# First-layer rows loaded one group ahead on another queue, one normalisation moved, one warm-up product added

## The chip, the cores and the metric

One core of a Trainium2 chip runs the whole program. The metric is device microseconds of one execution; the median of the runs counts. Engines and queues are named as in the profile: PE is TensorE, PEld its weight loads, DVE is VectorE, ACT is ScalarE, POOL is GpSimd, SP is SyncE, which here only starts transfers. A transfer is started from SP's queue or from ACT's queue.

## The reference

A two-layer encoder on 256 tokens of width 2048, all in float32:

```
for l in range(DEPTH):                                   # DEPTH = 2
    h = rms_norm(x, norm1_g[l])
    q, k, v, gu, gv = jnp.split(h @ w_in[l], splits, axis=-1)
    q = apply_rope(rms_norm(q, q_norm_g[l]), cos, sin)   # 8 query heads of 128
    k = apply_rope(rms_norm(k, k_norm_g[l]), cos, sin)   # 2 key/value heads
    attn = banded_window_attention(q, k, v, sink[l])
    sgu = chunked_spatial_gating(gelu(gu), gelu(gv), sgu_ln_g[l], sgu_ln_b[l], w_s[l], b_s[l])
    mixed = concatenate([rms_norm(attn, attn_out_g[l]), rms_norm(sgu, sgu_out_g[l])], axis=-1)
    x = x + mixed @ w_o[l]
    x = x + conv_gated_ffn(rms_norm(x, norm2_g[l]), w_up[l], conv_w[l], conv_b[l], w_down[l])
```

The RMS norms divide each row by the root of its mean square. Since that factor is one number per row, the kernel multiplies the unscaled rows by the weights and applies the factor to the product.

## The kernel before

Each product is made from three: an operand is split into a high part, rounded to a shorter float32 format, and a low part, the rest; high times high, low times high and high times low are added up in PSUM. Weights arrive by SP's queue in blocks of 1 MB (`raw`, three buffers), ACT makes the high part (`hi`, L128) and DVE the low part (`lo`, L110), each in two halves of 128x1024, with four half buffers each. PE needs one block for 24 products of 512 columns.

The work around the change has three places.

**The start.** `first_rows(b)` (L510) makes the operands of one of four groups of rows of the transposed input `xT`: for group 0 from the two tiles `xs` loaded at the very start, for groups 1 to 3 from two tiles of 256 KB that it loads itself on SP's queue (L515). ACT makes the high part of each 128-row piece (L246) and DVE its low part (L247). The first layer's loop at L548 calls it for group b and then multiplies that group with two weight blocks, one of the keys and values (`psk`) and one of the first four query heads (`psq`). I number the weight blocks 0, 1, 2 and so on; group b meets blocks 2b and 2b+1. Before the first weights land, PE multiplies a constant tile with itself nine times (L97, `WARM`). In group 1 ACT's queue loads the rotary tables `ropes` (L555), the norm gains `qk` (L334) and the column parameters `pc` (L335), in group 2 the residual `xr` in two halves of 1 MB (L559). In the last group DVE makes the rotary tables times gains (L343, L345) and the negated sinks (L353), and ACT sums the squares of the residual (L306).

**The attention half's norm.** `inv_rms_cols(acca, ...)` (L287) adds the sums of squares of the attention output on DVE (L288), and puts a piece of work called `turned` on a list. `let_in` takes such a piece off the list at a fixed point of the next block of products: it turns the sums with two PE transposes (L294), reduces them on DVE (L296), and POOL takes the power. It is called at L681, between the first and second unit of the gating half (`gated(0)` and `gated(1)`), so `let_in` of `gated(1)` takes it in. Its result `ra` is used by the first residual of the output projection (L530).

**The spatial products.** `spatial(u)` (L653) uses a PSUM buffer of the same two-buffer pool (`tp`) as the attention's transposes and L294.

What sets the order: the program is written out once, a scheduler orders each engine's instructions by readiness and priority (`urgent` raises it, `issue_after` binds a piece behind a named instruction), and on the chip each engine runs its own list in that order. Transfers use eight completion semaphores in turn, so a transfer may wait for the landing of the one that last used its semaphore.

## Time and profile before

| | |
|---|---|
| Median of 3 runs | 2008.98 us (2008.42 to 2009.18) |
| Profiled execution: its time, its span | 2008.75 us, 2007.0 us |
| PE busy | 2000.7 us (100%) |
| DVE busy | 1367.1 us (68%) |
| ACT busy | 1068.1 us (53%) |
| Transfers | 382.22 MB, mean 190 GB/s |
| First 10 us, 10 to 20 us, 20 to 30 us | 239, 413, 411 GB/s |

The span runs from the first instruction of the program to the last; the profiled execution took 1.75 us more than its span. A row of the timeline gives start and duration in us, engine, line, operation, tiles, count, and in brackets the idle time of the engine before it and what ended that. Blocks of rows that follow one another on an engine are merged.

### The profile page before, as it was taken

How to read it: one execution, taken by the hardware profiler on the slowest of the kernel's cores; microseconds unless marked ns; L12 is line 12 of the kernel's file. 1: busy time of each engine (PE TensorE's matmuls, PEld its weight loads, DVE VectorE, ACT ScalarE, POOL GpSimd, SP SyncE). 2: the span in 40 equal slices, each digit the busy share in tenths (PEclk: the TensorE clock that was granted, in tenths of full speed). 3: DMA queues.
4: the chain of work that ended last, by engine and by line, in shares of the span. 5: the costliest groups of instructions: out<-in, count | busy, mean ns of one | idle time of the engine just before them, and what ended most of it. 6: DMA issues, size and time to landing. Idle time of an engine off the chain costs nothing.

```text
span 2007.0 us, 26356 instructions
## 1 busy us (share of the span) xinstructions
PE 2000.7 (100%) x10426; PEld 1718.6 (86%) x10426; DVE 1367.1 (68%) x1866; ACT 1068.1 (53%) x1460; POOL 20.4 (1%) x25
## 2 busy tenths in 40 slices
PE   9999999999999999999999999999999999999999
PEld 7888888888888888888888888888888888888887
DVE  6878666777755577775567786667777444777753
ACT  6576465555543455555455764655555334555532
POOL 0100000000000000000000000000000000000000
PEclk9999999999999999999999999999999999999999
DMA  8644645455555544555556355544555554455563
GB/s 336 228 147 147 209 157 200 168 181 214 205 198 189 186 171 171 211 209 189 189 186 231 127 173 187 182 173 169 210 208 192 194 199 172 168 194 208 207 210 126
DMA packets 58011, 382.22 MB, mean 190 GB/s; under 512 B 6688, under 2 KB 7968, under 8 KB 12832
## 3 DMA queue, kind: packets, MB, share of 16 engines
q1 hardware_dynamic: 56880, 377.72, 53.2%
q10 hardware_dynamic: 1008, 2.83, 0.4%
q8 instruction: 81, 1.33, 0.3%
q14 instruction: 42, 0.34, 0.0%
HBM read 378.43 MB, written 2.10 MB: 190 GB/s over the span
## 4 chain that ended last, share of the span: by engine, by line
PE 97%; DMA 2%; DVE 1%; issue 0%; ACT 0%; SPq 0%; POOL 0%; DVEq 0%; ACTq 0%
PE mm L166 40%; PE mm L225 30%; PE mm L231 16%; PE mm L202 4%; PE mm L207 2%; PE tp L166 1%; DMA raw<-in_w_in 1%; PE tp L501 1%; DMA sl<-in_xT 1%; PE tp L463 0%; PE tp L266 0%; PE tp L653 0%; DVE lo L110 0%; PE tp L268 0%; PE tp L267 0%
## 5 line engine op out<-in xcount | busy, mean ns | idle before, releaser
L110 DVE TENSOR_TENSOR lo<-raw,hi 128x1024 fp32r<-128x1024 f32 (+1 forms) x708 | 840.5, 1215 | 445.1 <-ACT hi L128 287.6
L128 ACT ACTIVATE hi<-raw 128x1024 fp32r<-128x1024 f32 (+1 forms) x708 | 732.6, 1051 | 673.0 <-PE mm L166 374.3
L166 PE MATMUL mm<-hi,sl 128*128 128x512 f32 x2480 | 668.0, 391 | 0.7 <-ACT sl L246 0.7
L225 PE MATMUL mm<-sl,hi 128*128 128x512 f32 x2688 | 617.8, 389 | 0.0
L225 PEld LDWEIGHTS mm<-sl,hi 128*128 128x128 f32 x2688 | 501.8, 188 | 103.4 <-ACT hi L128 1.0
L166 PEld LDWEIGHTS mm<-hi,sl 128*128 128x128 f32 x2480 | 463.9, 188 | 96.4 <-ACT sl L246 1.1
L166 PE MATMUL mm<-lo,sl 128*128 128x512 f32 x1240 | 382.9, 390 | 0.0
L231 PEld LDWEIGHTS mm<-sl,lo 128*128 128x128 f32 x2688 | 328.1, 192 | 3.3
L231 PE MATMUL mm<-sl,lo 128*128 128x256 f32 x2688 | 329.1, 283 | 0.0
L166 PEld LDWEIGHTS mm<-lo,sl 128*128 128x128 f32 x1240 | 232.5, 188 | 48.1
L731 DVE SCALAR_TENSOR_TENSOR sc<-ev,pc,sc 128x255 f32<-128x255 f32 x176 | 80.9, 481 | 87.4 <-ACT sc L730 87.4
L239 ACT COPY ev<-mm 128x512 f32<-128x512 f32 x96 | 55.4, 577 | 130.6 <-PE mm L231 114.8
L730 ACT ACTIVATE sc<-ev,pc 128x256 f32<-128x256 f32 x176 | 98.9, 589 | 0.0
L202 PE MATMUL mm<-sl,hi 128*128 128x512 f32 x384 | 92.8, 392 | 0.0
L734 DVE SCALAR_TENSOR_TENSOR sc<-ev,pc,sc 128x255 f32<-128x255 f32 x176 | 80.9, 481 | 3.0
L202 PEld LDWEIGHTS mm<-sl,hi 128*128 128x128 f32 x384 | 70.8, 188 | 13.8
L254 ACT ACTIVATE sl<-sl 128x256 fp32r<-128x256 f32 x88 | 31.8, 409 | 68.3 <-DVE sl L751 68.3
L241 DVE TENSOR_TENSOR ev<-mm,ev 128x512 f32<-128x512 f32 x96 | 65.7, 684 | 0.0
L726 DVE TENSOR_TENSOR ev<-ev,rb 128x512 f32<-128x512 f32 x88 | 60.1, 683 | 0.2
L207 PE MATMUL mm<-sl,lo 128*128 128x256 f32 x384 | 50.4, 284 | 0.0
L207 PEld LDWEIGHTS mm<-sl,lo 128*128 128x128 f32 x384 | 48.3, 191 | 0.9
L255 DVE TENSOR_TENSOR sl<-sl 128x256 fp32r<-128x256 f32 x88 | 33.5, 421 | 20.1 <-ACT sl L254 20.1
(122 smaller groups left out, 692.3 us busy)
## 6 DMA issues: line engine op xcount, KB each, us to landing
raw<-in_w_up SPq DMA_DIRECT2D x176, 1024.0 KB, 5.1
raw<-in_w_down SPq DMA_DIRECT2D x88, 1024.0 KB, 4.8
raw<-in_w_in SPq DMA_DIRECT2D x38, 1024.0 KB, 5.0
raw<-in_w_o SPq DMA_DIRECT2D x32, 1024.0 KB, 4.9
raw<-in_w_gu SPq DMA_DIRECT2D x16, 1024.0 KB, 4.8
sl<-in_prow SPq DMA_DIRECT2D x12, 256.0 KB, 6.2
raw<-in_w_in SPq DMA_DIRECT2D x8, 256.0 KB, 5.2
xr<-in_x ACTq DMA_DIRECT2D x2, 1024.0 KB, 8.8
```

Source lines behind the costliest of these rows:

```text
L110: nc.vector.tensor_tensor(out=lo, in0=part, in1=hi.bitcast(F32), op=ALU.subtract)
L128: nc.scalar.activation(hi[:, cs], part, AF.Copy)
L166: nc.tensor.matmul(ps[m], acts[kk][:, part % 2, m * P : (m + 1) * P], w, start=first and kk == 0 and part == 0, stop=last and kk == KB - 1 ...
L202: nc.tensor.matmul(ps[:, i, :], tile_of(his, k, i), x1, start=k == 0, stop=False)
L207: nc.tensor.matmul(ps[:, i, :SEQ], tile_of(los, k, i), acts[k][:, 0, :], start=False, stop=k == NK - 1)
L225: nc.tensor.matmul(pss[n][:, i, :], hs[k // KB][:, c : c + P], x1, start=k == 0, stop=False)
L231: nc.tensor.matmul(pss[n][:, i, :SEQ], los[k // KB][:, c : c + P], acts[k][:, 0, :], start=False, stop=k == len(acts) - 1)
L241: nc.vector.tensor_tensor(out=s, in0=ps[:, :, :SEQ], in1=rest, op=ALU.add)
L726: nc.vector.tensor_tensor(out=s, in0=s, in1=r2b2[0], op=ALU.mult)
L730: nc.scalar.activation(t[:, i, :], s[:, i, :], AF.Identity, bias=col(3), scale=col(1))
L731: nc.vector.scalar_tensor_tensor(out=t[:, i, 1:], in0=s[:, i, : SEQ - 1], scalar=col(0), in1=t[:, i, 1:], op0=ALU.mult, op1=ALU.add)
L734: nc.vector.scalar_tensor_tensor(out=t[:, i, : SEQ - 1], in0=s[:, i, 1:], scalar=col(2), in1=t[:, i, : SEQ - 1], op0=ALU.mult, op1=ALU.add)
```

## The change

Four edits. `xT`'s tiles for group b+1 are loaded when group b's operands are made, from ACT's queue instead of SP's, bound behind the last ACT instruction so far. The transfers of rope tables, gains and parameters stay in group 1 and on ACT's queue, and those of the residual move from group 2 to group 3. The call for the attention half's sums moves to just ahead of the output projection, so they are turned inside its first block pair. And ten constant products are made instead of nine.

```diff
-WARM = 9
+WARM = 10
...
+    def load_behind(pairs):
+        with tc.issue_after(latest(mybir.EngineType.Activation)):
+            for dst, src in pairs:
+                nc.scalar.dma_start(dst, src)
+
     def first_rows(b):
         with urgent():
             for j in (2 * b, 2 * b + 1):
-                if b:
-                    t = sl([P, 2, SEQ])
-                    nc.sync.dma_start(t, xT[:, 2 * j : 2 * j + 2, :])
-                else:
-                    t = xs[j]
                 for i in range(2):
                     c = C_N1 + 2 * j + i
-                    hT.append(split_act(t[:, i, :], pc[:, c : c + 1]))
+                    hT.append(split_act(xs[j][:, i, :], pc[:, c : c + 1]))
+            if b + 1 < NB:
+                new = [sl([P, 2, SEQ]) for _ in range(2)]
+                load_behind([(t, xT[:, 2 * j : 2 * j + 2, :]) for j, t in enumerate(new, 2 * b + 2)])
+                xs.extend(new)
...
                 first_rows(b)
-
-                with tc.issue_after(latest(mybir.EngineType.Activation)):
-                    if b == 1:
-                        ropes = const.tile([P, 2, 2, HD], F32, tag="ropes", name="ropes")
-                        nc.scalar.dma_start(ropes, rope)
-                        qk = layer_params_rest(0, pc, nc.scalar)
-                    if b == 2:
-                        for m in range(2):
-                            nc.scalar.dma_start(xr[:, m, :], x[:, m, :])
+                if b == 1:
+                    ropes = const.tile([P, 2, 2, HD], F32, tag="ropes", name="ropes")
+                    qk = lay.tile([P, 264], F32, tag="qk", name="qk")
+                    load_behind([(ropes, rope), (qk, prow[0:1, 0:264].partition_broadcast(P)), (pc[:, C_CW:], pcol[0, :, C_CW:])])
+                if b == 3:
+                    load_behind([(xr[:, m, :], x[:, m, :]) for m in range(2)])
...
         gated(0)
-        ra = inv_rms_cols(acca, D // 2, "a")
         gated(1)
...
+        ra = inv_rms_cols(acca, D // 2, "a")
         for c in range(4):
```

How the instructions stand on the engines, at three places. First ACT near the start, before: the rows from the last piece of group 0 (`sl_149`) on; `raw_108` and `raw_109` are weight blocks 0 and 1, `raw_245` block 2, `sl_224` and `sl_232` the two tiles of group 1.

```order
L246 ACTIVATE sl_149<-sl_107,pc_92 128x256
L128 ACTIVATE hi_158<-raw_108 128x512
L128 ACTIVATE hi_188<-raw_109 128x512 x2
L128 ACTIVATE hi_194<-raw_109 128x512 x2
L246 ACTIVATE sl_226<-sl_224,pc_92 128x256
L246 ACTIVATE sl_229<-sl_224,pc_92 128x256
L128 ACTIVATE hi_247<-raw_245 128x1024
L128 ACTIVATE hi_251<-raw_245 128x1024
L246 ACTIVATE sl_234<-sl_232,pc_92 128x256
L246 ACTIVATE sl_237<-sl_232,pc_92 128x256
L555 DMA ropes_240<-in_rope 128x512
```

The same place now; `sl_153` and `sl_154` are the tiles of group 1, `sl_241` and `sl_242` those of group 2, `raw_250` is block 2.

```order
L514 DMA sl_153<-in_xT 128x512
L128 ACTIVATE hi_163<-raw_109 128x512
L514 DMA sl_154<-in_xT 128x512
L128 ACTIVATE hi_193<-raw_110 128x512 x2
L128 ACTIVATE hi_199<-raw_110 128x512 x2
L246 ACTIVATE sl_229<-sl_153,pc_92 128x256
L246 ACTIVATE sl_232<-sl_153,pc_92 128x256
L246 ACTIVATE sl_235<-sl_154,pc_92 128x256
L246 ACTIVATE sl_238<-sl_154,pc_92 128x256
L514 DMA sl_241<-in_xT 128x512
L514 DMA sl_242<-in_xT 128x512
L128 ACTIVATE hi_252<-raw_250 128x1024
```

Both pieces of both tiles of group 1 now stand ahead of block 2's high parts, where the second tile's stood behind them, and ACT starts the tiles of the next group in between.

Second, DVE where the rotary tables are made, before; `raw_590` is block 8, `raw_487` block 7.

```order
L110 TENSOR_TENSOR lo_490<-raw_487,hi_489 128x1024
L247 SCALAR_TENSOR_TENSOR sl_409<-sl_407,pc_92,sl_409 128x256
L247 SCALAR_TENSOR_TENSOR sl_412<-sl_407,pc_92,sl_412 128x256
L110 TENSOR_TENSOR lo_494<-raw_487,hi_493 128x1024
L110 TENSOR_TENSOR lo_593<-raw_590,hi_592 128x1024
L343 TENSOR_TENSOR sl_431<-ropes_240,qk_242 128x128
L345 TENSOR_TENSOR sl_431<-ropes_240,qk_242 128x64 x2
```

And now, the end of the piece: `raw_368` is block 5, `raw_454` block 6, `qk_246` the first layer's gains and `qk_2525` the second layer's, which SP loads.

```order
L247 SCALAR_TENSOR_TENSOR sl_411<-sl_331,pc_92,sl_411 128x256
L110 TENSOR_TENSOR lo_375<-raw_368,hi_374 128x1024
L343 TENSOR_TENSOR sl_432<-ropes_245,qk_246 128x128
L345 TENSOR_TENSOR sl_432<-ropes_245,qk_246 128x64 x2
...
L345 TENSOR_TENSOR sl_439<-ropes_245,qk_246 128x64 x2
L353 TENSOR_SCALAR nsink_446<-qk_246 128x8
L353 TENSOR_SCALAR nsink_8872<-qk_2525 128x8
L110 TENSOR_TENSOR lo_457<-raw_454,hi_456 128x1024
```

The tables and both rows of negated sinks stood behind block 8's first low part; they now stand ahead of block 6's.

Third, PE at the end of the first layer's attention, before:

```order
L267 MATMUL tp<-sl 128x512
L268 MATMUL tp<-sl 128x512
L202 MATMUL mm<-sl,hi 128x512 x4
L207 MATMUL mm<-sl,lo 128x256 x13
L294 MATMUL tp<-ident,sl 128x128 x2
L653 MATMUL tp<-sl,vn 128x128 x8
L207 MATMUL mm<-sl,lo 128x256 x11
L653 MATMUL tp<-sl,vn 128x128 x4
```

And now (L655 is the old L653):

```order
L268 MATMUL tp<-sl 128x512
L655 MATMUL tp<-sl,vn 128x128 x8
L202 MATMUL mm<-sl,hi 128x512 x4
L207 MATMUL mm<-sl,lo 128x256 x18
L655 MATMUL tp<-sl,vn 128x128 x4
L207 MATMUL mm<-sl,lo 128x256 x6
L655 MATMUL tp<-sl,vn 128x128 x4
L207 MATMUL mm<-sl,lo 128x256 x8
```

The two transposes L294 have left this place; they come after six of the eight steps of the output projection's first chunk. The first two spatial products follow the attention's last product at once. The second layer has the same moves.

## The prediction

> **What bounds the kernel now.** I read the page's busy shares first, then its chain of work that ended last, then who PE waited for, and at last the timeline around each wait.

> ```profile
> PE 2000.7 (100%) x10426; PEld 1718.6 (86%) x10426; DVE 1367.1 (68%) x1866; ACT 1068.1 (53%) x1460; POOL 20.4 (1%) x25
> PE 97%; DMA 2%; DVE 1%; issue 0%; ACT 0%; SPq 0%; POOL 0%; DVEq 0%; ACTq 0%
> 297.18 14.53 PE mm L225 x64
> 311.72 7.67 PE mm L231 x64
> ```

> PE is busy for 2000.7 of 2007.0 us and holds 97% of the chain. In steady state a product of 512 columns takes 14.53/64 = 0.227 us and one of 256 takes 7.67/64 = 0.120. No edit removes a product, so the change can win only what PE loses between products. All idle time is 2007.0 - 2000.7 = 6.3 us, and part of that is the first microsecond and the store at the end. The waits on PE name two places that the change touches:

> ```profile
> PE mm L166 <- ACT sl L246: 0.7, 1, 0.7
> PE tp L294 <- DVE sl L288: 0.2, 1, 0.2
> ```

> The first is in block 6, the keys' block of group 3. PE's timeline, the chain and ACT's timeline show it:

> ```profile
> 39.96 1.07 PE L166 MATMUL mm<-hi,sl 128*128 128x512 f32 x4
> 40.87 0.61 PE L166 MATMUL mm<-lo,sl 128*128 128x512 f32 x2
> 42.14 1.48 PE L166 MATMUL mm<-hi,sl 128*128 128x512 f32 x4 [0.65 <-ACT sl L246]
> ...
> 31.38 10.17 DMA sl<-in_xT
> ...
> 41.58 0.91 ACT L246 ACTIVATE sl<-sl,pc 128x256 fp32r<-128x256 f32 x2 [4.89 <-DMA sl<-in_xT]
> ```

> Six products take 1.36 us, so the step after 39.96 was due at 41.32. It began at 42.14, 0.82 late, and its four high products took 1.48 instead of 1.07, 0.41 more, since the low half of the rows came later still. The loss is 1.23 us. Its cause is the last tile of xT: started at 31.38, landed 41.55.

> **The change part by part.** *Rows one group ahead.* Group 3's tiles are now started while group 2's operands are made and are not behind the residual, which moves after them; the second starts with block 4's second high part:

> ```profile
> 22.96 1.04 ACT L128 ACTIVATE hi<-raw 128x1024 fp32r<-128x1024 f32 x1
> ```

> From 23 us, even at the 10.17 us of the row above it lands by 33.2, eight ahead of 41.3. So I take off the whole 1.23 us; bounds 0 (the tiles are still late) and 1.23.

> What it puts in instead is at block 2, the first with a moved tile ahead of it.

> ```profile
> 9.20 1.92 ACT L128 ACTIVATE hi<-raw 128x512 fp32r<-128x512 f32 x3 [0.35 <-DMA raw<-in_w_in]
> 12.44 0.91 ACT L246 ACTIVATE sl<-sl,pc 128x256 fp32r<-128x256 f32 x2
> 15.05 1.06 ACT L128 ACTIVATE hi<-raw 128x1024 fp32r<-128x1024 f32 x1 [1.70 <-DMA raw<-in_w_in]
> 15.62 0.33 ACTq L555 DMA_DIRECT2D ropes<-in_rope  x1
> ...
> 16.15 2.36 DVE L110 TENSOR_TENSOR lo<-raw,hi 128x1024 fp32r<-128x1024 f32 x2 [2.20 <-ACT hi L128]
> ...
> 16.84 1.07 PE L166 MATMUL mm<-hi,sl 128*128 128x512 f32 x4
> 17.75 0.62 PE L166 MATMUL mm<-lo,sl 128*128 128x512 f32 x2
> ...
> 7.57 7.38 DMA raw<-in_w_in
> ...
> L515 SPq DMA_DIRECT2D sl<-in_xT x1: 328/328/328, 8.3 to 8.3; - x1
> ...
> DMA to landing us min/median/max: 7.3/7.3/7.3
> ...
> 8.00:41.00 33.00, 33.00 (x147) 27.26 (x146) 21.86 (x30) 19.32 (x28) 0.00 (x0) 1.00 1.02 407
> ```

> Block 2 lands at 7.57 + 7.38 = 14.95, its first low part is done at 16.15 + 1.2 = 17.35, and PE uses that at 17.75: only 0.4 us of slack. From 8 to 41 us the transfers run at their full share (1.02, 407 GB/s), so order decides. Before, the second tile of group 1 (started 8.3, 7.3 us to landing: 15.6) followed block 2; now it runs beside or ahead of it, and block 2 is the one that lands at 15.6. Then high part 15.7 to 16.8, low part to 18.0. PE, late by 0.23 for another reason below, needs it at 17.98. I put 0.1 us for this wait.

> The other condition is that ACT has made group 1's four pieces by 15.6, as they now stand ahead of block 2. The second pair takes 0.91, so the second tile must land by 14.7. Its transfer can start behind the activation that begins at 9.20.

> ```profile
> ropes<-in_rope ACTq DMA_DIRECT2D x1, 256.0 KB, 6.0
> raw<-in_w_in SPq DMA_DIRECT2D x8, 256.0 KB, 5.2
> ```

> By the nearest row, 256 KB pieces in the same stretch, 5.2 us, it lands at 14.4; by that of the rope table on ACT's queue beside 1 MB loads, 15.2; by the old 7.3, 16.5. The wait is then 0, 0.5 or 1.8 us. I take the nearest row. The last is the end of the range.

> SP loses six starts and ACT gains six of 0.33 us (the rope row at 15.62, which ran while the activation of 15.05 to 16.11 executed). They cost nothing as long as ACT's engine has work in hand; the two of group 1 could each delay a high part of the first blocks, by at most 0.33 us.

> [...] Were the queues separate, block 2 would land at 14.95 as before, and the 0.1 us would be zero.

> *Tables ahead of block 6.* DVE now makes the rope tables before block 6's low parts, which PE needs at 39.51:

> ```profile
> 38.60 1.07 PE L166 MATMUL mm<-hi,sl 128*128 128x512 f32 x4
> 39.51 0.62 PE L166 MATMUL mm<-lo,sl 128*128 128x512 f32 x2
> ...
> 45.75 0.28 DVE L343 TENSOR_TENSOR sl<-ropes,qk 128x128 f32<-128x128 f32 x1
> 47.21 1.22 DVE L110 TENSOR_TENSOR lo<-raw,hi 128x1024 fp32r<-128x1024 f32 x1
> ...
> qk<-in_prow ACTq DMA_DIRECT2D x1, 132.0 KB, 6.3
> ```

> Three quarters of the tables took 45.75 to 47.21, so all take 2.0 us, then 1.2 for the low part: the gains must land by 36.3. They are started once group 3's last piece is handed to ACT. That tile starts at 23 and at 5.2 to 7.3 us (the rows above) lands by 28.2 to 30.3; the gains, 6.3 later, by 34.5 to 36.6. With less traffic then than at 16 us, since the residual now comes behind them, I take no wait. The bound is a tile that needs 10.17: gains at 39.5, a wait of 3.2 us. Queued behind it on DVE are six low parts.

> *The attention half's sums.* Before, PE stood for a chain that ends in DVE's addition:

> ```profile
> 174.91 0.60 ACT sl L471
> 176.92 0.44 DVE sl L288
> ...
> 175.62 1.71 PE L207 MATMUL mm<-sl,lo 128*128 128x256 f32 x13
> 177.49 0.30 PE L294 MATMUL tp<-ident,sl 128*128 128x128 f32 x1 [0.16 <-DVE sl L288]
> ...
> 1175.52 1.83 PE L207 MATMUL mm<-sl,lo 128*128 128x256 f32 x14
> 1177.44 0.41 PE L294 MATMUL tp<-ident,sl 128*128 128x128 f32 x2
> ```

> Thirteen products from 175.62 end at 177.18 and L294 began at 177.49: 0.31 lost; in the second layer 1175.52 + 14 x 0.120 = 1177.20 against 1177.44: 0.24. The chain now ends some 14 us before its user. In L294's old place stand spatial products, whose second PSUM buffer is freed by the copy that starts at 174.91 and takes 0.60, while the first spatial product still runs, so I expect no new wait. Gain 0.55; bounds 0 (L294 waits as long for a PSUM buffer in its new place) and 0.55.

> *One more constant product.*

> ```profile
> 1.05 3.91 PEld L97 LDWEIGHTS tp<-ones 128*128 128x128 f32 x18 [1.05 <-DVE ones L93]
> 4.91 2.04 PE L166 MATMUL mm<-hi,sl 128*128 128x512 f32 x4
> 6.76 0.66 PE L166 MATMUL mm<-lo,sl 128*128 128x512 f32 x2
> 7.26 1.09 PE L166 MATMUL mm<-hi,sl 128*128 128x512 f32 x4
> ```

> Nine products are 18 passes in 3.91 us, 0.217 each, and the first real product follows at once, at 4.91. A tenth puts it 0.43 later. The first four real products take 1.85 us, the next four 0.9: PE runs at half pace until about 6.7. If that moment stays, one slow product fewer fits ahead of it, which costs 0.23. If the pace follows the number of passes instead, the cost is 0.43 less the 0.46 - 0.23 saved on each of two products, about 0. I take 0.23, as PE is busy without a break from 1.05 either way; upper bound 0.43, lower 0.

> **The sum.** -1.23 - 0.55 + 0.10 + 0.23 = -1.45 us. The span goes from 2007.0 to 2005.6, the profiled execution from 2008.75 to 2007.3. The median lies 0.23 above the profiled execution: 2008.98 - 1.45 = 2007.5.

> **The rivals.** *A, the rows arrive late for block 2, slower.* The second tile lands at 16.5: 1.8 us lost in block 2. The next group's first tile starts only then: at 6.0 it lands at 22.5, its two pieces (0.9) and block 3's high and low part (1.06 and 1.2) end at 25.7, and PE, 24 products of 0.227 after 17.98 + 1.8, needs that at 25.2: 0.5 more. -1.23 - 0.55 + 0.23 + 2.3 = +0.75: 2009.7. It turns slower than before when the tile lands after 15.7. For it speaks the 7.3 of the old row, against it that the tiles no longer stand behind a 1 MB load on their own queue.

> *B, DVE stands at the tables, slower.* 3.2 us before block 6's low parts: 2010.7, slower from 1.45 us on, that is from gains that land after 37.7. For it speaks that two transfers must land first, the second layer's gains too; against it the lighter traffic.

> *C, the transposes keep their wait in the new place,* as DVE frees their PSUM buffer late: 2008.0.

> **How the numbers follow.** Chances: forecast 0.66, A 0.18, B 0.06, C 0.10. The range 2006.4 to 2009.7 holds forecast, C and most of A. The likeliest case's own is 2006.6 to 2008.3: the sum's bounds at block 2 and at the constant product (0 to 0.5 and 0 to 0.43) and the runs before, which spread over 0.8 us. A measurement here tells 0.2%, 4.0 us, from no change. Faster by that needs more than twice the sum, of 6.3 us in all: 0.03. Slower by that needs A and B together and more: 0.03. Within: 0.94.

> **What would show it.** Right: no wait of PE on L246 near 41, none before L294 near 177 and 1177, the first real product at about 5.3, PE whole from 16 to 20. A wait of PE on `lo` or `hi` at 17 to 25 says A; on `lo` near 40, with DVE waiting for `qk` or `ropes`, B. The forecast is wrong if PE's idle time does not fall by one to two microseconds, or if it falls and the time does not.

## The result and the profile after

| | before | after |
|---|---|---|
| Median, measured side by side | 2008.51 us (2007.17 to 2009.18) | 2013.88 us (2012.89 to 2015.06) |
| Profiled execution: its time, its span | 2008.75, 2007.0 us | 2013.99, 2012.2 us |
| PE busy | 2000.7 us | 2002.1 us |

The change makes the kernel slower by 5.4 us: the ratio is 1.0027, with a 95% interval of 1.0018 to 1.0036. Forecast was 2007.5 us, with a range up to 2009.7.

The waits on PE name one place that was not there before. The two that the change was to remove (L246 near 41 us and L294) are gone from the list.

```profile
PE mm L166 <- ACT hi L128: 4.7, 1, 4.7
```

PE's timeline shows it at the start of block 2:

```profile
5.34 1.44 PE L166 MATMUL mm<-hi,sl 128*128 128x512 f32 x4
...
16.61 0.61 PE L166 MATMUL mm<-lo,sl 128*128 128x512 f32 x2
21.89 2.07 PE L166 MATMUL mm<-hi,sl 128*128 128x512 f32 x4 [4.67 <-ACT hi L128]
23.76 1.05 PE L166 MATMUL mm<-lo,sl 128*128 128x512 f32 x2
24.62 1.91 PE L166 MATMUL mm<-hi,sl 128*128 128x512 f32 x4
26.32 0.66 PE L166 MATMUL mm<-lo,sl 128*128 128x512 f32 x2
26.82 1.09 PE L166 MATMUL mm<-hi,sl 128*128 128x512 f32 x4
```

Block 2 was due at 16.61 + 2 x 0.227 = 17.06 and began at 21.89, 4.83 us late. Then something follows that the wait does not explain: the ten products that begin between 21.89 and 26.32 take 4.43 us instead of 10 x 0.227 = 2.27, so 2.16 us more are lost. The table by stretches shows that PE had its operands there but not its clock (columns: busy time and instructions of PE, PEld, DVE, ACT and POOL, then the granted clock, the transfers' share and GB/s):

```profile
12.00:16.00 4.00, 4.00 (x20) 3.30 (x19) 1.05 (x2) 0.33 (x1) 0.00 (x0) 1.00 1.00 404
16.00:22.00 6.00, 1.33 (x7) 0.80 (x5) 1.90 (x5) 3.03 (x6) 0.00 (x0) 0.80 0.89 310
22.00:27.00 5.00, 5.00 (x13) 3.95 (x14) 4.04 (x5) 3.60 (x6) 0.00 (x0) 0.56 0.48 151
...
41.00:44.00 3.00, 3.00 (x15) 2.49 (x14) 2.87 (x14) 1.33 (x2) 0.00 (x0) 1.00 1.00 423
```

From 22 to 27 us PE is busy all the time and makes 13 products at a granted clock of 0.56. From 41 to 44 it is busy without a gap: the loss that the change was to remove there is gone.

What released PE, by ACT's timeline and by the chain of waits:

```profile
16.28 0.91 ACT L246 ACTIVATE sl<-sl,pc 128x256 fp32r<-128x256 f32 x2 [3.95 <-DMA sl<-in_xT]
19.36 0.51 ACT L246 ACTIVATE sl<-sl,pc 128x256 fp32r<-128x256 f32 x1 [2.17 <-DMA sl<-in_xT]
...
20.78 2.00 ACT L128 ACTIVATE hi<-raw 128x1024 fp32r<-128x1024 f32 x2 [0.51 <-DVE sl L247]
```

```profile
9.05 10.29 DMA sl<-in_xT
...
19.36 0.52 ACT sl L246
...
19.91 0.89 DVE sl L247 x2
20.80 1.05 ACT hi L128
```

ACT stood 3.95 us for group 1's first tile and 2.17 us more for the second, which landed only at 19.34. Block 2 itself had landed at 16.07; its high parts waited behind the four pieces on ACT's list.

Why a tile of 256 KB took 10.29 us is in the transfers from 12 to 16 us, by queue (packets, MB, share of the 16 engines). Here q10 is ACT's queue and q1 SP's. First before, then after:

```profile
q1 hardware_dynamic: 338, 1.70, 101.8%
```

```profile
q1 hardware_dynamic: 169, 1.25, 76.1%
q10 hardware_dynamic: 197, 0.36, 24.0%
```

The two queues moved about as many packets, but not bytes. A packet is one partition's row: 8 KB of a weight block (0.31 us each in the trace), 2 KB of a tile of rows (0.08 us). If the queues take turns packet by packet, a tile of 128 packets needs as many turns as a 1 MB block of 128 packets, and lands with it. That is what the landings show: first tile 16.26 and block 2 16.07, second tile 19.34 and block 3 19.16.

The landings alone would also fit longer turns, of eight rows, a transfer's share on one of the 16 engines if they share it evenly (128 rows over 16). The single packet records of the trace from 11.5 to 16 us settle that. The end of a weight row and the start of a tile row coincide to 10 ns 223 times, where chance gives 73 (the next steps of 10 ns to either side); the end of a weight row and the start of another do so 64 times, where chance gives about 53. So the two kinds alternate row by row.

The loss adds up, in one execution against the other: -1.23 (near 41 us) - 0.55 (L294) + 0.22 (the first product of block 2 was due at 17.06 and began before at 16.84) + 4.83 + 2.16 = +5.4 us; the spans differ by 5.2.

### The profile page after: what moved, and what is told of

It reads as the page before. It is cut to its first block, busy times and chain, and to the rows that moved or that the text cites. A ratio compares the mean times of both kernels' runs of the same rounds, so it can differ in the third digit from the quotient of the medians.

```text
span 2012.2 us, 26364 instructions
## 1 busy us (share of the span) xinstructions
PE 2002.1 (99%) x10428; PEld 1720.5 (86%) x10428; DVE 1366.6 (68%) x1866; ACT 1069.0 (53%) x1460; POOL 20.4 (1%) x25
## 4 chain that ended last, share of the span: by engine, by line
PE 98%; DMA 1%; DVE 1%; ACT 0%; SPq 0%; issue 0%; POOL 0%; DVEq 0%; ACTq 0%
PE mm L166 42%; PE mm L225 30%; PE mm L231 16%; PE mm L202 4%; PE mm L207 2%; PE tp L166 1%; PE tp L501 1%; DMA sl<-in_xT 1%; PE tp L463 0%; PE tp L266 0%; PE tp L655 0%; PE tp L267 0%; PE tp L268 0%; DMA raw<-in_w_in 0%; DVE lo L110 0%; PE tp L414 0%
## 5 line engine op out<-in xcount | busy, mean ns | idle before, releaser
L110 DVE TENSOR_TENSOR lo<-raw,hi 128x1024 fp32r<-128x1024 f32 (+1 forms) x708 | 840.4, 1215 | 446.2 <-ACT hi L128 283.5
L128 ACT ACTIVATE hi<-raw 128x1024 fp32r<-128x1024 f32 (+1 forms) x708 | 732.7, 1052 | 673.5 <-PE mm L166 381.0
L166 PE MATMUL mm<-hi,sl 128*128 128x512 f32 x2480 | 669.5, 391 | 4.8 <-ACT hi L128 4.7
L225 PE MATMUL mm<-sl,hi 128*128 128x512 f32 x2688 | 617.2, 390 | 0.0
L225 PEld LDWEIGHTS mm<-sl,hi 128*128 128x128 f32 x2688 | 502.1, 188 | 102.5
L166 PEld LDWEIGHTS mm<-hi,sl 128*128 128x128 f32 x2480 | 464.6, 188 | 100.5 <-ACT hi L128 5.6
L166 PE MATMUL mm<-lo,sl 128*128 128x512 f32 x1240 | 383.5, 390 | 0.0
L231 PEld LDWEIGHTS mm<-sl,lo 128*128 128x128 f32 x2688 | 328.1, 192 | 3.3
L231 PE MATMUL mm<-sl,lo 128*128 128x256 f32 x2688 | 329.1, 283 | 0.0
L166 PEld LDWEIGHTS mm<-lo,sl 128*128 128x128 f32 x1240 | 233.0, 188 | 48.6
L207 PE MATMUL mm<-sl,lo 128*128 128x256 f32 x384 | 50.4, 285 | 0.0
L207 PEld LDWEIGHTS mm<-sl,lo 128*128 128x128 f32 x384 | 48.3, 191 | 0.9
## 6 DMA issues: line engine op xcount, KB each, us to landing
sl<-in_prow SPq DMA_DIRECT2D x12, 256.0 KB, 6.3
raw<-in_w_in SPq DMA_DIRECT2D x8, 256.0 KB, 4.9
```

The lines of the kernel that those rows point to most:

```text
L110: nc.vector.tensor_tensor(out=lo, in0=part, in1=hi.bitcast(F32), op=ALU.subtract)
L128: nc.scalar.activation(hi[:, cs], part, AF.Copy)
L166: nc.tensor.matmul(ps[m], acts[kk][:, part % 2, m * P : (m + 1) * P], w, start=first and kk == 0 and part == 0, stop=last and kk == KB - 1 ...
L207: nc.tensor.matmul(ps[:, i, :SEQ], tile_of(los, k, i), acts[k][:, 0, :], start=False, stop=k == NK - 1)
L225: nc.tensor.matmul(pss[n][:, i, :], hs[k // KB][:, c : c + P], x1, start=k == 0, stop=False)
L231: nc.tensor.matmul(pss[n][:, i, :SEQ], los[k // KB][:, c : c + P], acts[k][:, 0, :], start=False, stop=k == len(acts) - 1)
```

## The experiments

My theory after the result had three parts: **turns** (a small packet on one queue costs the same turn as a large one on the other), **list** (ACT works in order, so block 2's high parts stand behind pieces that wait), and **clock** (the long idle time of PE lowers its granted clock afterwards). Each median is compared with the kernel before in the same series of runs.

| | median, us | over the kernel before, us | ratio, 95% |
|---|---|---|---|
| 20 constant products in the gap | 2013.31 | +4.5 | 1.0014 to 1.0032 |
| second tile's pieces behind block 2 | 2009.81 | +1.0 | 0.9996 to 1.0015 |
| a group as one transfer | 2010.36 | +1.5 | 0.9997 to 1.0016 |
| a group as four transfers | 2016.22 | +7.4 | 1.0023 to 1.0049 |
| loads alone | 2013.62 | +5.3 | 1.0016 to 1.0034 |
| sums alone | 2007.47 | -0.9 | 0.9987 to 1.0005 |
| group 1 on SP's queue, ten products | 2013.52 | +5.2 | 1.0015 to 1.0035 |
| the same, nine products | 2014.02 | +5.7 | 1.0017 to 1.0036 |
| and pieces bound, ten products | 2008.26 | -0.3 | 0.9990 to 1.0008 |
| before, sums moved, residual last | 2012.58 | +4.1 | 1.0012 to 1.0029 |
| pieces and tables bound, ten products | 2007.60 | -0.9 | 0.9985 to 1.0003 |
| the same, nine products | 2007.89 | -0.7 | 0.9988 to 1.0006 |

### The clock: PE kept busy in the gap

The change, with 20 constant products on PE between blocks 1 and 2. They add no work to the result.

```diff
             in_rows([psk[:, m, :] for m in range(2)], 2, b)
             in_rows([psq[:, m, :] for m in range(2)], 0, b)
+            if l == 0 and b == 0:
+                with tc.issue_after(latest()), urgent():
+                    fill = tp([P, P])
+                    for _ in range(FILL):
+                        nc.tensor.matmul(fill, ones, ones, start=True, stop=True)
```

> The changed kernel with 20 more constant products on PE between weight blocks 1 and 2, where PE stood for 4.67 us; nothing else changed. Theory (the wait let PE's granted clock fall, and that costs 2.0 us by itself): block 2 still starts at about 21.9 us, since ACT and the transfers do the same, but its first ten products go at 0.23 us each instead of 0.43, and the time falls by about 2.0 us, to 2011.9. Rival (the ten slow products are slow because their operands come late, in small pieces): they stay at 0.43 us and the time stays at 2013.9.

PE's timeline:

```profile
17.08 4.63 PE L575 MATMUL tp<-ones 128*128 128x128 f32 x40
21.77 1.21 PE L167 MATMUL mm<-hi,sl 128*128 128x512 f32 x4
...
39.97 0.74 PE L167 MATMUL mm<-lo,sl 128*128 128x512 f32 x2 [0.32 <-DVE lo L111]
```

Block 2 begins at the same time (21.77), but its products run at 0.227 us: four in 1.21 us instead of 2.07. All ten executions show a mean granted clock of 1.000, where the changed kernel's eight show 0.998 or 0.999. So the slow products came from PE's idle time, not from the late operands. Yet the median falls only from 5.4 to 4.5 us over the kernel before (the profiled span by 0.7), not by 2. Comparing PE's losses place by place in the two profiled executions, the 2.16 us are won back; 0.45 of it is lost again inside block 2, 0.41 at 164 us, 0.13 at the start, and 0.48 at 39 us, where block 6's first low part comes late. DVE's timeline names that one:

```profile
38.58 0.17 DVE L354 TENSOR_SCALAR nsink<-qk 128x8 f32<-128x8 f32 x1 [3.90 <-DMA qk<-in_prow]
38.69 4.63 DVE L111 TENSOR_TENSOR lo<-raw,hi 128x1024 fp32r<-128x1024 f32 x4
```

It is rival B of the prediction, in a small size: a tiny operation on the second layer's gains stands ahead of block 6's low parts. In the changed kernel PE was late enough to hide it.

### The list: the second tile's pieces behind block 2's high parts

Same transfers; only the order on ACT and DVE differs.

```diff
         his, los = split_weights(src, raw)
+        while late:
+            with tc.issue_after(latest(mybir.EngineType.Activation)), urgent():
+                split_act(*late.pop(0)[1:], late_t.pop(0))
...
-                    hT.append(split_act(xs[j][:, i, :], pc[:, c : c + 1]))
+                    if b and j % 2:
+                        t = sl([P, 2, SEQ], F32R)
+                        hT.append(t)
+                        late_t.append(t)
+                        late.append((t, xs[j][:, i, :], pc[:, c : c + 1]))
+                    else:
+                        hT.append(split_act(xs[j][:, i, :], pc[:, c : c + 1]))
```

> The changed kernel, but the pieces of each group's second tile stand on ACT and DVE behind the high parts of the next weight block instead of ahead of them. Transfers of group 1 as before. Theory (ACT runs its list in order, so block 2's high parts stand behind a tile that PE needs only 2.7 us later): the second tile still lands at about 19.3, block 2's first high part is ready at 18.2, PE waits 1.3 instead of 4.7 us and keeps its pace, so 3.4 + 2.0 us come back: 2008.5. Rival (the tile itself is what PE lacks): PE starts block 2 early but stops in its middle until 21 us or later, the pace falls anyway, and the time is 2012 to 2014.

```profile
18.88 1.20 PE L170 MATMUL mm<-hi,sl 128*128 128x512 f32 x4 [1.31 <-ACT hi L128]
20.14 0.73 PE L170 MATMUL mm<-lo,sl 128*128 128x512 f32 x2
```

The second tile still lands at 19.38, but PE waits 1.31 us instead of 4.67, and its pace stays whole. So 3.4 us of wait were ACT's list, and about 2 us the clock that went with it. The median is 1.3 us above what I expected (2009.81, not 2008.5). In the profiled execution, 2009.21, a weight piece that came late at 8.1 us, before the place of the change, cost 0.8. And the pace was not whole in every execution: three of the ten show a mean clock of 0.999 and took 2010.7 to 2012.0.

### The turns: larger and smaller packets

A group's 512 KB in one transfer with 4 KB per partition, and in four with 1 KB. The one transfer goes into a tile of its own, and the pool `slots` has one buffer less for it.

```diff
-    slots = pool("slots", 43)
+    slots = pool("slots", 42)
+    xgp = pool("xgp", 1)
...
-                new = [sl([P, 2, SEQ]) for _ in range(2)]
-                load_behind([(t, xT[:, 2 * j : 2 * j + 2, :]) for j, t in enumerate(new, 2 * b + 2)])
-                xs.extend(new)
+                wide = xgp.tile([P, 4, SEQ], F32, tag="xg", name="xg")
+                load_behind([(wide, xT[:, 4 * b + 4 : 4 * b + 8, :])])
+                xs.extend(wide[:, 2 * i : 2 * i + 2, :] for i in range(2))
```

> The changed kernel, but the two tiles of a group are one transfer with 4 KB per partition instead of two with 2 KB (128 packets instead of 256, the same bytes; one slot buffer fewer). Theory (the two queues take turns packet by packet, so a packet of 2 KB costs as long a turn as one of 8 KB, and 128 packets take as long as one weight block): group 1 lands when block 2 does, at about 16.3, its four pieces end at 18.2, PE waits about 2.4 instead of 4.7 us, and the time is 2009.5 to 2011.5. Rival (the queues share bytes, or the tile is late only because it is started late): the 512 KB land at 19.3 as before and the time stays at 2013.9.

```diff
-                load_behind([(t, xT[:, 2 * j : 2 * j + 2, :]) for j, t in enumerate(new, 2 * b + 2)])
+                load_behind([(t[:, i, :], xT[:, 2 * j + i, :]) for j, t in enumerate(new, 2 * b + 2) for i in range(2)])
```

> The changed kernel, but a group is loaded by four transfers with 1 KB per partition instead of two with 2 KB (512 packets instead of 256, the same bytes). Theory (turns by packet): the group needs the turns of four weight blocks; only blocks 2 and 3 are under way, so half of it is still to come when block 3 lands at 19.2, and the last piece lands at 20.5 to 22; the time rises by 1 to 3 us, to 2015 to 2017. Rival (shared bytes, or a late start): the last piece lands at 19.3 and the time stays at 2013.9.

ACT's and PE's rows of the one transfer:

```profile
17.48 1.70 ACT L247 ACTIVATE sl<-xg,pc 128x256 fp32r<-128x256 f32 x4 [4.82 <-DMA xg<-in_xT]
```

```profile
20.18 1.20 PE L167 MATMUL mm<-hi,sl 128*128 128x512 f32 x4 [2.98 <-ACT hi L129]
21.44 1.22 PE L167 MATMUL mm<-lo,sl 128*128 128x512 f32 x2
22.46 1.91 PE L167 MATMUL mm<-hi,sl 128*128 128x512 f32 x4
```

And ACT's and PE's of the four:

```profile
12.42 0.50 ACT L246 ACTIVATE sl<-sl,pc 128x256 fp32r<-128x256 f32 x1
16.27 0.51 ACT L246 ACTIVATE sl<-sl,pc 128x256 fp32r<-128x256 f32 x1 [3.35 <-DMA sl<-in_xT]
19.14 0.51 ACT L246 ACTIVATE sl<-sl,pc 128x256 fp32r<-128x256 f32 x1 [2.37 <-DMA sl<-in_xT]
21.95 0.51 ACT L246 ACTIVATE sl<-sl,pc 128x256 fp32r<-128x256 f32 x1 [2.29 <-DMA sl<-in_xT]
```

```profile
23.52 2.08 PE L166 MATMUL mm<-hi,sl 128*128 128x512 f32 x4 [6.51 <-ACT hi L128]
```

The same bytes are there at 17.45, 19.34 or 21.92 us, in packets of 4, 2 and 1 KB. A piece of 128 KB in 1 KB packets lands 2.8 us after the one before it, just as a tile of 256 KB in 2 KB packets lands 3.1 us after its forerunner: each with one weight block (the last three with blocks 2, 3 and 4, at 16.03, 18.91 and 21.73). So it is the number of packets, not of bytes, that sets a tile's landing beside a full queue of larger packets. The one transfer landed 1.65 us behind block 2, not with it, as I had expected: 126 of its 128 packets had started by 15.8 us, when block 2 landed, and the last two followed 0.46 us apart, which is one packet of each kind (0.31 and 0.16 us).

The profiled execution of the one transfer is the slowest of its ten. The four with a mean clock of 1.000 took 2008.6 to 2010.1 us, the six with 0.999 took 2010.1 to 2011.9: so the clock fell in some executions and not in others.

### Which edit carries the loss

The loads alone are the changed kernel with the sums at their old place and nine constant products:

```diff
-WARM = 10
+WARM = 9
...
         gated(0)
+        ra = inv_rms_cols(acca, D // 2, "a")
         gated(1)
...
-        ra = inv_rms_cols(acca, D // 2, "a")
         for c in range(4):
```

> The change's loads alone: the attention half's sums at their old place, nine constant products. Theory (the whole loss is made by group 1's second tile, which gets one packet's turn for each of the larger packets of the weights, and by the four pieces of rows that stand ahead of block 2's high parts on ACT): PE waits 4.5 to 5.1 us for block 2's first high part, its next ten or so products take 0.43 us each, and the waits before L294 near 177 and 1177 are back; 5.4 + 0.55 - 0.2 = 5.8 us over the kernel before. Rival (the tenth product or the moved sums carry part of the loss): under 5 us over the kernel before.

And the sums alone are the kernel before with this edit only:

```diff
         gated(0)
-        ra = inv_rms_cols(acca, D // 2, "a")
         gated(1)
...
+        ra = inv_rms_cols(acca, D // 2, "a")
         for c in range(4):
```

> The kernel before with the attention half's sums turned in the output projection, nothing else. Theory: the waits of 0.32 and 0.24 us before L294 near 177 and 1177 go, nothing takes their place: 0.55 us under the kernel before, and in the timeline no loss of PE from 170 to 185 and 1170 to 1185. Rival (the transposes wait as long in the new place, or the spatial products now wait): no difference, and a wait of 0.2 or more at the new place.

The loads alone lose 5.3 us, as much as the whole change and 0.5 less than expected: the wait is 4.08 us, not 4.5 to 5.1. In PE's timeline block 2 stands in the same way, and the waits before L294 are back (0.32 and 0.23 us):

```profile
21.05 2.08 PE L166 MATMUL mm<-hi,sl 128*128 128x512 f32 x4 [4.08 <-ACT hi L128]
22.93 1.05 PE L166 MATMUL mm<-lo,sl 128*128 128x512 f32 x2
23.78 1.15 PE L166 MATMUL mm<-hi,sl 128*128 128x512 f32 x4
```

Six products are slow here, not ten. With the sums alone PE loses nothing around 177 and 1177 us, so the forecast gain of 0.55 us is there; the median is 0.9 us lower, which these runs cannot tell from 0.55. Its timeline also shows that the gap near 41 us differs between executions, with the same loads as before:

```profile
40.88 0.61 PE L166 MATMUL mm<-lo,sl 128*128 128x512 f32 x2
41.43 1.49 PE L166 MATMUL mm<-hi,sl 128*128 128x512 f32 x4
```

The late group was due at 41.33; it begins 0.1 late and loses 0.42 inside. That is 0.5 us, where the execution that I had read lost 1.23.

### Group 1 on SP's queue

```diff
-                load_behind([(t, xT[:, 2 * j : 2 * j + 2, :]) for j, t in enumerate(new, 2 * b + 2)])
+                pairs = [(t, xT[:, 2 * j : 2 * j + 2, :]) for j, t in enumerate(new, 2 * b + 2)]
+                if b == 0:
+                    for dst, src in pairs:
+                        nc.sync.dma_start(dst, src)
+                else:
+                    load_behind(pairs)
```

> The change, but group 1's two tiles are started on SP's queue ahead of block 2; groups 2 and 3 stay on ACT's queue, one group ahead. Theory (turns by packet between the queues, and ACT's list): group 1's tiles land by 13, so ACT makes their pieces before block 2 lands; block 2 lands 0.6 to 1.3 us later than the 14.95 of the kernel before; PE waits 0.1 to 1.5 us for it and keeps its full pace; the waits near 41 and before L294 stay away: -1.23 - 0.55 + 0.2 + 0.1 to 1.5 = 1.5 to 0 us under the kernel before. Rival (loading one group ahead crowds block 2 out, whichever queue starts it): a PE wait of over 3 us at block 2, reduced pace behind it, and 3 us or more over the kernel before.

And with nine constant products:

```diff
-WARM = 10
+WARM = 9
```

> As the kernel with group 1 on SP's queue, but nine constant products instead of ten. Theory (the pace of the first real products follows the time since PE began, so a tenth product only takes the place of slow real ones): the first real product at 4.91 instead of 5.34, one or two slow products more, time within 0.3 us of the kernel with ten. Rival (the tenth product costs its whole 0.43 us): 0.43 us less than with ten.

I was wrong: with group 1 on SP's queue the kernel is 5.2 us over the kernel before (5.7 with nine products). In the run with ten, group 1's tiles landed by 12.17 and block 2 at 15.98, but ACT's timeline shows who stood ahead of block 2 now:

```profile
19.25 0.91 ACT L246 ACTIVATE sl<-sl,pc 128x256 fp32r<-128x256 f32 x2 [4.97 <-DMA sl<-in_xT]
20.07 1.99 ACT L128 ACTIVATE hi<-raw 128x1024 fp32r<-128x1024 f32 x2
```

These are pieces of group 2. The scheduler had put them, which are `urgent`, ahead of block 2's high parts; their tile, on ACT's queue, landed at 19.23. The trap had moved by one group. Alone, this result would also fit the rival, that the early loads crowd the weights out, so I separated the two by the list alone:

```diff
     def first_rows(b):
-        with urgent():
+        with ExitStack() as order, urgent():
+            if b > 1:
+                order.enter_context(tc.issue_after(latest(mybir.EngineType.Activation)))
```

> As the kernel with group 1 on SP's queue and ten constant products, but the pieces of groups 2 and 3 are bound behind the last high part of the weight block ahead of their own group; no piece stands ahead of block 2's high parts any more that waits for a tile on ACT's queue. Theory (what cost 4 us there was ACT's list, which stood for group 2's first tile, landed 19.23, while block 2 had landed at 15.98): block 2's high parts run from about 16 us, PE waits 0 to 0.5 us for them or the first low part, full pace throughout, no gap near 41 and none before L294: -1.23 - 0.55 + 0.2 + 0.2 = 1.4 us under the kernel before. Rival (the tiles on ACT's queue themselves slow the weights by that much): a PE wait of over 3 us at block 2 or 3 and over 3 us above the kernel before.

The same transfers on the same queues, but the pieces of groups 2 and 3 behind the block before them: -0.3 us instead of +5.2, where 1.4 under was expected. The rival falls. PE loses 0.2 us at block 2, and 0.94 at block 3, for a reason that DVE's timeline shows:

```profile
24.50 0.74 PE L166 MATMUL mm<-lo,sl 128*128 128x512 f32 x2 [0.78 <-DVE lo L110]
```

```profile
23.11 0.17 DVE L353 TENSOR_SCALAR nsink<-qk 128x8 f32<-128x8 f32 x1 [4.05 <-DMA qk<-in_prow]
23.22 2.36 DVE L110 TENSOR_TENSOR lo<-raw,hi 128x1024 fp32r<-128x1024 f32 x2
```

A 0.17 us operation on the gains stood 4.05 us at the head of DVE's list, ahead of block 3's low parts. I bound it, with the tables, behind block 5's last low part:

```diff
-                tabs, nsink = rope_tables(qk, ropes)
+                with tc.issue_after(latest(mybir.EngineType.DVE)):
+                    tabs, nsink = rope_tables(qk, ropes)
```

> As the kernel with group 1 on SP's queue and bound pieces, and the rotary tables with the negated sinks are bound behind block 5's last low part on DVE. Theory (the 0.9 us that PE lost near 23 is DVE's list: the small operation on the gains stood ahead of block 3's low parts and the gains landed at 23.09): that loss goes, the full pace stays, no gap near 41: 0.9 us less than with the tables unbound, 1.2 to 2.2 us under the kernel before by the profiled spans. Rival (block 3's low parts were late because block 3 itself was, at 18.51): the loss near 23 stays.

The last kernel is the same with `WARM = 9`.

> The same with nine constant products. Theory (PE works without a break from 1.05 us on, so the tenth product moves the first real one by 0.43 and takes the place of slow ones, by where the change of pace happens to fall): first real product 0.1 to 0.45 us earlier than with ten, time within 0.4 us of it, either sign. Rival (the tenth product is needed for the pace): the first products of block 0 slow for 1 us longer and the time over 0.4 us longer.

The loss near 23 is gone. By the table of stretches of the kernel with ten, PE works from 8 to 45 us without a gap and at full clock:

```profile
8.00:24.00 16.00, 16.00 (x72) 13.17 (x71) 13.10 (x21) 12.64 (x21) 0.00 (x0) 1.00 1.00 395
24.00:45.00 21.00, 21.00 (x94) 17.38 (x94) 13.52 (x26) 11.96 (x22) 0.00 (x0) 1.00 1.00 396
```

PE reaches the attention (its first L463 transpose near 163 us) 1.5 us earlier than without the bound tables, more than the 0.9 expected, and is still 1.5 ahead at 1162 us. But the profiled spans are nearly alike, 2006.4 and 2006.5, so that this one is 0.6 us under the kernel before and not 1.2 to 2.2: from 1695 to 1808 us this execution loses 1.5 us in the second layer's L225 products. Other executions lose there too, in other sizes (0.5 us in that of before, 0.1 with the tables unbound), so I don't put it down to the edit; the cause wasn't followed.

With ten products its median is 0.9 us under the kernel before, with a ratio of 0.9994 and an interval of 0.9985 to 1.0003 that holds 1. So with the lists mended the same loads lose nothing that can be measured; whether they win the forecast 1.5 us is below what these runs tell. With nine constant products the first real product comes at 4.89 as with ten, and the medians (2007.60, 2007.89) do not differ beyond their spread. With group 1 on SP's queue and no binding, nine gave 5.00 against 5.34 and a median 0.5 higher, also inside the spread. So the tenth product neither gains nor costs anything that these runs can tell.

### The residual's place

The kernel before with the sums moved and the residual started in group 3; all tiles of rows on SP's queue as before.

```diff
-                    if b == 2:
+                    if b == 3:
                         for m in range(2):
                             nc.scalar.dma_start(xr[:, m, :], x[:, m, :])
```

> The kernel before with two edits only: the sums turned in the output projection, and the residual's two transfers started in group 3 instead of group 2; all tiles of rows stay on SP's queue as before, nine constant products. Theory (the last tile took 10.17 us because its 2 KB packets took turns with the residual's 8 KB packets on the other queue): without the residual beside it the last tile lands before 39, the gap near 41 goes, 1.23 + 0.55 = 1.8 us under the kernel before, no other wait. Rival (the tile is late because SP starts it late, behind the weights): the gap near 41 stays, 0.55 us under the kernel before.

The gap near 41 us goes, and the rival with it: the last tile is started at 31.08, as late as before, and lands at 37.37, after 6.3 us instead of 10.17. So the residual beside it made it late; that would hold for queues that share bytes as well as for turns. But the median is 4.1 us over the kernel before, which neither side expected. The chain of waits and PE's timeline:

```profile
44.50 8.89 DMA xr<-in_x
...
60.27 0.72 POOL xr L283
```

```profile
61.03 0.43 PE tp L320 x2
```

In the profiled execution, whose span is 3.1 us longer than before, PE stood 2.6 us for the rows' norm, which needs the squares of the whole residual; its second half was started at 44.50 and landed at 53.39. Seven of the eleven executions also show a mean clock below 1.000 and took 2012.2 to 2014.0 us, the other four 2010.5 to 2012.0. The rest of the loss wasn't followed. In the changed kernel the residual's halves start at 36.51 and 40.22 and land by 50.05, and PE does not wait at L320. The move has a deadline that the prediction did not price; from the landing to L320 the chain took 7.6 us, so by my estimate from 50.05 it is done by about 57.7, ahead of the 59.50 at which L320 runs in the changed kernel, 6 us later than in the kernel before (53.44).

## Why the prediction was wrong

**What failed** is the term for block 2, +0.10, and in it the choice "I take the nearest row": 5.2 us for 256 KB pieces, hence a landing at 14.4. Those pieces were of 2 KB packets with nothing on the other queue after 3.4 us. The tile landed at 19.34, 10.29 us after its start. A row quoted in the prediction itself came near that price: the last tile of `xT`, 10.17 us, landing while residual and weights came on two queues. From 9.05 it gives 19.2. That it fits so closely is luck, since that tile stood behind a 1 MB block on its own queue; but it showed how long 256 KB can take beside a queue of 8 KB packets. I used it as an upper bound for group 3 and not for group 1, where a 1 MB block on the other queue was certain. The alternative bounds were short too. The old place (7.3) had no second queue beside it. The rope table (6.0) did stand on ACT's queue, but all its packets moved from 19 to 21 us, when SP's queue moved 160 packets of only 0.42 MB, most of them as small as its own. A row must be chosen by what shares the engines with it, packet by packet, not by size: the same 512 KB landed here at 17.45, 19.34 or 21.92 us in packets of 4, 2 and 1 KB.

The prediction counted the move in bytes: block 2 at 15.6, where the tile had landed before, or at 14.95 were the queues separate. Block 2 landed at 16.07, started 0.8 us later than before (8.39 for 7.57). The queues did share, and by packets: from 12 to 16 us SP's queue moved 169 packets and 1.25 MB instead of 338 and 1.70 MB, beside 197 packets and 0.36 MB on ACT's queue, and a turn was one row.

**The rest of the block-2 step was right in kind.** The condition that ACT must have made the four pieces first, since they stand ahead of block 2 on its list, is what decided; a landing at 19.34 instead of 14.7 means 4.64 us, and PE lost 4.83. Rival A named mechanism and place, and was sized by the old 7.3.

**No term existed for the clock.** Ten products at 0.43 us, 2.16 us lost in all, are in no case of the prediction. Its first-product rows already showed PE at half pace until it had worked for some time (1.85 us for the first four products, 0.9 for the next); I did not ask what a long wait would do to that. Nothing in the trace of before has PE wait for more than 0.7 us once it has started.

**What held.** The gap near 41 us is gone (-1.23, though another execution with the old loads lost only 0.5 there), L294 no longer waits (-0.55, and no wait in the new place, so C falls), the first real product came at 5.34, and block 2 was due 0.22 later, for 0.23 forecast. These make -1.56, and they are lost in 4.83 + 2.16 = +7.0. B's place shows as 0.48 us once PE is earlier, in the run with filled gap, not as 3.2. That B cost nothing in the changed kernel is luck: the gains landed at 40.60 there, later than the 37.7 from which B was to make it slower and not at 34.5 to 36.6, and it was PE's lateness of 7 us that hid it. The statement of what would show it was right: a wait of PE on `hi` at 17 to 25 said A.

**What stays open.** The pace of the first products differs between executions by itself (with nine constant products the first four took 2.04 us in the kernel before and 1.17 in the last kernel of the experiments; PE's granted clock rises at 6.81 us in the kernel before, at 5.93 in the changed one), so terms of 0.2 to 0.4 us there can't be settled by single profiles. That the number of slow products after a wait of about 4 us is six in two kernels and ten and thirteen in two others fits where the wait lies on the clock's grid (last section); no run moved a wait along that grid on purpose.

## What to carry to other kernels

When a transfer is moved to another queue, count its packets against those of the transfer that runs beside it: with small packets beside large ones it landed here when as many large ones had gone, however few its bytes (two tiles of 256 KB at 16.26 and 19.34 us, the 1 MB blocks beside them at 16.07 and 19.16). Ask of every instruction that waits for such a transfer what stands behind it on its engine's list; three times here (rows on ACT, one group on and again; gains on DVE) a short piece of work that was put early, because it was expected to be ready, held work whose data had landed. And count a wait of some microseconds on TensorE at more than its length: 4.67 us of it were followed here by products at a granted clock of 0.50, which lost 2.16 us more.

## What was not expected of the hardware

The granted clock after a wait, in the profiled executions: with PE idle for 1.3 us (second tile's pieces late) no run of slow products followed; with 2.98 us eight were, with 4.67 ten, with 6.51 twelve, each 0.43 us instead of 0.227. After the 2.98 us the first four products still ran at full pace (1.20 us together, as after the 1.3 us), and the slow ones began 1.3 us after the restart.

The table of stretches of the changed kernel, cut in such steps:

```profile
16.17:19.58 3.41, 1.05 (x5) 0.55 (x3) 0.89 (x2) 1.12 (x3) 0.00 (x0) 1.00 0.89 309
19.58:22.99 3.41, 1.10 (x3) 0.91 (x4) 2.00 (x3) 2.69 (x4) 0.00 (x0) 0.50 0.81 282
22.99:26.40 3.41, 3.41 (x10) 2.64 (x9) 2.45 (x5) 2.21 (x4) 0.00 (x0) 0.50 0.36 83
26.41:29.82 3.41, 3.41 (x17) 2.78 (x16) 3.41 (x5) 2.83 (x5) 0.00 (x0) 1.00 1.02 351
```

PE was busy for 1.05 us of the first step, and the clock is 0.50 in the next; it was busy for 1.10 of that, and the clock stays at 0.50; then it was busy for all of a step, and the clock is back at 1.00. For the other runs I counted the same steps back from where PE's rows come back to full pace, which is an estimate: near 23.9 us with the loads alone, 24.0 with group 1 on SP's queue, 26.6 with nine products there, 24.8 with one transfer, 28.9 with four. By it the clock fell after steps with PE busy for 0 to 1.2 us and stayed full after about 1.8 (four transfers); once at half, it rose after steps with PE busy for about 2.9 us (the loads alone, group 1 on SP's queue) and not after 2.0 (four transfers) or 2.5 (nine products). So, by this count, the clock was at half for one step with the loads alone and with group 1 on SP's queue (six slow products), and for two in the changed kernel and with nine products there (ten and thirteen). It fits, too, that the slow products began only 1.3 us after the restart in the run with 2.98 us of wait: a step ended about there. No run changed PE's busy time within a step on purpose.

Of packets, in the changed kernel: 2 KB took 0.08 us and 8 KB 0.31 us, and a row of the one kind was mostly followed by a row of the other (223 coincidences where chance gives 73).
